# Making the low part of streamed fp32 weights by an accumulating DMA in place of a GpSimd subtraction

## The chip, the cores and the metric

The kernel runs on one core of a Trainium2 chip. The metric is the device time of one execution in microseconds (us). The time of the kernel before is the median of three runs.

## The reference

One inference step of a two-layer trunk in fp32, for a prompt of 16 + 1024 tokens and for eight sample sequences of eight tokens each. Layer 0 mixes tokens by gated DeltaNet, layer 1 by RWKV-7; both are wrapped in RMSNorm and a residual add. Cut to its dense products, which are what the change touches:

```python
# layer 0, D = 1024, 16 value heads of 128
xn   = rmsnorm(x, norm_w[0])
proj = xn @ w_in                        # 1024 x 6176: q, k, v, z and two gates
qkv, z = causal_conv(proj[..., :4096]), proj[..., 4096:6144]
o    = delta_rule(qkv, gates)           # chunked, state 128 x 128 for each head
x    = x + (rmsnorm(o) * silu(z)) @ w_out           # 2048 x 1024
# layer 1, 16 heads of 64
xn   = rmsnorm(x, norm_w[1])
r, k, v, z = [mix(xn, i) @ w_rkvz[i] for i in range(4)]   # 4 x 1024 x 1024
y    = wkv(r, k, v, decay, a)           # state 64 x 64 for each head
x    = x + (groupnorm(y) * silu(z)) @ w_o           # 1024 x 1024
```

## The kernel before, in words

All 1104 tokens (64 of the samples, 16 meta, 1024 of the prompt) stand as columns in three segments of 384, 384 and 336. Activations lie in SBUF as a high part, rounded to the `fp32r` type that TensorE reads, and a low part, the rest. A dense product sums three products, high weight by high activation, low weight by high activation and high weight by low activation, into one PSUM tile (`dense`, line 208; `dense3`, line 1067, for some projections).

Weights are streamed by `load_w` (line 189). A *weight tile* is 128 output columns; it comes in *halves* of four contraction blocks, each a tile of 128 partitions by 4 x 128 numbers (256 KB). For each half:

- SyncE loads the raw fp32 half from DRAM into `wraw` (line 197, two buffers);
- ScalarE casts it to the high part `whi` (line 82 in `split`, three buffers);
- GpSimd subtracts, raw less high, into the low part `wlo` (line 86 in `split`, three buffers).

With three buffers for the low part, the second half of a tile takes the buffer of the first half of the tile before. A buffer is free when TensorE has used it in the last of the three segments. Calls of `load_w` with `into` (16 halves of the second part of `gdn_w_out`, and two halves that are loaded again) let VectorE subtract, into tiles that stay; the change leaves them as they are. Without `into` there are 260 halves: 96 of `gdn_w_in`, 20 of `gdn_w_out`, 96 of `rwkv_w_rkvz` and 48 of `rwkv_w_o`. Four of the 20 are the two tiles that the second part of `gdn_w_out` starts with.

The stages in order: the input's norm; for each of eight pairs of heads `j` the projections for keys (PSUM tile `dk`), queries (`dq`), two values (`dv`) and two gates (`dz`), between which the inverse of a triangular matrix runs on VectorE (`inverse32`, lines 439 and 441) and the recurrence of the pair before on all engines; the output projection (`d`, lines 906 and 914); the norm and token shift of layer 1; the RWKV projections (`project`, line 1138); the gates (`rwkv_gates`, line 1020: `dz` for the first segment, `zz` for the others, one segment at a time); the RWKV recurrence with the output projection (`project_out`, line 1521) interleaved; the final norm.

The order of the instructions on each engine is not written out by hand: the kernel is built with a scheduler that plans it from its own cost model (`schedule_with_timeline_sim=True`, line 1779). Each engine then runs its list in order and waits at its head. So an instruction that comes late holds up all that stands behind it on its engine, and a change of one instruction's planned cost reorders the rest.

Of the kernel before, what the change touches and what calls it, by code (L numbers as in the profile page):

```python
# [10 lines left out]
AF = mybir.ActivationFunctionType  # L11
ALU = mybir.AluOpType
# [23 lines left out]
class Builder:  # L36
# [152 lines left out]
    def load_w(self, src, kt=8, into=None):  # L189

        nc = self.nc
        n = src.shape[1]
        v = src.rearrange("(k p) m -> p k m", p=128)
        his, los = [], []
        for h in range(0, kt, 4):
            w = self.t(self.wp, [128, 4, 128], "wraw", 2)
            nc.sync.dma_start(w[:, :, 0:n], v[:, h:h + 4, :])
            if into:
                hi, lo = into[0][h // 4], into[1][h // 4]
            else:  # L200
                hi = self.t(self.wp, [128, 4, 128], "whi", 3, F32R)
                lo = self.t(self.wp, [128, 4, 128], "wlo", 3, F32R)
            self.split(w[:, :, 0:n], hi[:, :, 0:n], lo[:, :, 0:n], eng_lo="dve" if into else "pool")
            his.append(hi)
            los.append(lo)
        return his, los
# [1576 lines left out]
```

## Time and profile before

| | |
|---|---|
| Median of three runs | 2455.74 us (2452.48 to 2456.87) |
| The profiled execution | 2463.55 us |
| Its span, first to last instruction | 2461.6 us |
| Granted TensorE clock, mean | 0.972 |
| Busy: TensorE, VectorE, ScalarE, GpSimd | 93%, 67%, 56%, 44% |
| Bytes moved by DMA | 284.66 MB, all from SyncE's queue but 3.38 MB of instructions |

PE is TensorE's matmul, PEld its weight load, DVE is VectorE, ACT ScalarE, POOL GpSimd, SP SyncE; a `q` behind the name is that engine's instruction queue. L86 is line 86 of the kernel. `wlo<-wraw,whi` names the tile written and those read, buffer numbers left out. A group's row has its count, its busy time in us, the mean of one in ns, the idle time of its engine just before it, and what ended most of that. In the timeline a row has start and duration in us; merged rows carry a count. The rows of a matmul overlap the next one's, since matmuls are pipelined: what counts for pace is the distance between two starts.

### The profile page before, as it was taken

What the parts mean: (1) busy time and instruction counts of PE and PEld (TensorE: products, weight loads), DVE (VectorE), ACT (ScalarE), POOL (GpSimd) and SP (SyncE); (2) the same over time, 40 slices, a digit from 0 to 9 for tenths busy, and PEclk for the clock granted to TensorE, in tenths of its full rate; (3) what the DMA queues carried; (4) which work ended last, traced back from release to release, by engine and by line L of the source; (5) the groups of instructions that cost most, each with busy time, mean ns of one, the idle gap of its engine ahead of it and who ended that gap; (6) DMA issues with size and microseconds to landing.
All of it is one profiled execution on the core that took longest, in us unless ns stands there. A gap on an engine that the chain in (4) does not pass through costs nothing. (4 is left out here: it accounts for less than half of the span.)

```text
span 2461.6 us, 52742 instructions
## 1 busy us (share of the span) xinstructions
PE 2285.6 (93%) x18593; PEld 2053.9 (83%) x18593; DVE 1657.3 (67%) x4364; ACT 1370.1 (56%) x3817; POOL 1090.5 (44%) x1478
## 2 busy tenths in 40 slices
PE   6989999999999999999999999988979999999996
PEld 5888989898988989889899998876758777877885
DVE  6878676876768586843358344788865687667563
ACT  5455546564555564664336465564434577677663
POOL 3435343433444343441315235433357565656653
PEclk9999999999999999999999999999989999999997
DMA  3323333333332424261531556667565443343331
GB/s 109 103 72 99 84 108 84 102 86 85 88 101 66 118 81 106 73 203 57 150 94 42 168 178 168 165 192 179 148 197 166 125 139 107 91 142 89 109 103 49
DMA packets 471939, 284.66 MB, mean 116 GB/s; under 512 B 187481, under 2 KB 457050, under 8 KB 471674
## 3 DMA queue, kind: packets, MB, share of 16 engines
q1 hardware_dynamic: 471674, 281.29, 40.5%
q8 instruction: 147, 2.41, 0.4%
q14 instruction: 118, 0.97, 0.1%
HBM read 200.00 MB, written 81.17 MB: 114 GB/s over the span
## 5 line engine op out<-in xcount | busy, mean ns | idle before, releaser
L86 POOL TENSOR_TENSOR wlo<-wraw,whi 128x512 fp32r<-128x512 f32 x260 | 349.0, 1346 | 369.4 <-ACT whi L82 334.9
L82 ACT CAST whi<-wraw 128x512 fp32r<-128x512 f32 x260 | 160.0, 617 | 162.0 <-PE dq L76 50.6
L76 PE MATMUL d<-xc,whi 128*128 128x384 f32 (+3 forms) x846 | 239.0, 340 | 1.8 <-ACT ev L1145 1.8
L406 DVE SCALAR_TENSOR_TENSOR cvy<-raw,cw,cvy 128x408 f32<-128x408 f32 (+2 forms) x288 | 176.7, 626 | 16.6 <-ACT cvy L62 14.8
L439 DVE TENSOR_TENSOR invtmp<-invA,invT 72x31 f32<-72x31 f32 (+31 forms) x403 | 163.5, 406 | 17.0 <-POOL invT L434 6.4
L441 DVE TENSOR_TENSOR invT<-invT,invtmp 72x31 f32<-72x31 f32 (+31 forms) x403 | 169.0, 419 | 6.4
L76 PEld LDWEIGHTS d<-xc,whi 128*128 128x128 f32 (+1 forms) x846 | 155.5, 191 | 9.6 <-issue 5.3
L76 PE MATMUL dz<-xc,whi 128*128 128x384 f32 (+1 forms) x480 | 149.5, 343 | 0.0
L76 PE MATMUL dv<-xc,whi 128*128 128x384 f32 (+1 forms) x480 | 146.7, 334 | 0.0
L76 PE MATMUL d<-xa,whi 128*128 128x384 f32 (+3 forms) x450 | 139.0, 342 | 3.4 <-ACT xa L82 2.5
L76 PE MATMUL dz<-xa,whi 128*128 128x384 f32 (+1 forms) x416 | 136.8, 350 | 2.9 <-ACT whi L82 2.6
L76 PE MATMUL d<-xc,wlo 128*128 128x384 f32 (+2 forms) x396 | 131.2, 341 | 0.0
L855 POOL TENSOR_SCALAR Sb<-Sb,eglb 128x128 f32<-128x128 f32 x128 | 80.2, 645 | 88.5 <-DMA Sb<-in_state_gdn 23.1
L76 PE MATMUL rA<-rS,AR 128*64 128x128 f32 x512 | 106.8, 291 | 7.4 <-DVE rS L1432 4.4
L76 PE MATMUL rA<-UV,G 128*64 128x64 f32 x1152 | 112.5, 223 | 0.4 <-ACT UV L62 0.4
L76 PEld LDWEIGHTS rA<-UV,G 128*64 128x64 f32 x1152 | 101.9, 139 | 3.2 <-issue 1.4
L76 PE MATMUL dv<-xa,whi 128*128 128x384 f32 (+1 forms) x288 | 99.9, 347 | 0.1
L62 ACT ACTIVATE rX<-rA,rk 64x64 f32<-64x64 f32 x272 | 83.6, 307 | 23.0 <-PE rA L76 17.1
L76 PE MATMUL dz<-xa,wlo 128*128 128x384 f32 (+1 forms) x256 | 89.8, 351 | 5.3 <-POOL wlo L86 5.3
L1432 DVE SCALAR_TENSOR_TENSOR rS<-rA,DC,pre 64x64 f32<-64x64 f32 x256 | 72.2, 282 | 28.2 <-PE rA L76 22.5
L76 PE MATMUL fG<-AR,BK 128*128 128x128 f32 x576 | 86.3, 288 | 4.4 <-DVE G L1366 2.3
L76 PEld LDWEIGHTS dz<-xc,whi 128*128 128x128 f32 x480 | 89.7, 192 | 0.8
(506 smaller groups left out, 7500.1 us busy)
## 6 DMA issues: line engine op xcount, KB each, us to landing
wraw<-in_gdn_w_in SPq DMA_DIRECT2D x96, 256.0 KB
wraw<-in_rwkv_w_rkvz SPq DMA_DIRECT2D x96, 256.0 KB
Sb<-in_state_gdn SPq DMA_DIRECT2D x64, 256.0 KB
wraw<-in_rwkv_w_o SPq DMA_DIRECT2D x48, 256.0 KB
E<-drow SPq DMA_DIRECT2D x24, 384.0 KB
attn<-drow SPq DMA_DIRECT2D x24, 384.0 KB
wraw<-in_gdn_w_out SPq DMA_DIRECT2D x36, 256.0 KB
out_s_gdn<-Sb SPq DMA_DIRECT2D x32, 256.0 KB
```

Of the source, the lines that this page charges most:

```text
L62: return self.nc.scalar.activation(out, in_, func, bias=bias, scale=scale, **kw)
L76: self.nc.tensor.matmul(out, lhsT, rhs, start=start, stop=stop)
L82: nc.scalar.copy(hi, x)
L86: e.tensor_tensor(lo, x, hi.bitcast(F32), op=ALU.subtract)
L406: nc.vector.scalar_tensor_tensor(y[:, 0:wd], raw[:, k:k + wd], cw[k], y[:, 0:wd], op0=ALU.mult, op1=ALU.add)
L439: nc.vector.tensor_tensor(tmp, A[:, j, j + 1:32].unsqueeze(2).broadcast_to([nb, n, m]), Tv[:, j, 0:m].unsqueeze(1).broadcast_to([nb, n, m] ...
L441: nc.vector.tensor_tensor(Tv[:, j + 1:32, 0:m], Tv[:, j + 1:32, 0:m], tmp, op=ALU.subtract)
L855: nc.gpsimd.tensor_scalar(Sb[:, u], Sb[:, u], self.eglb[:, hv, 4 * g + u:4 * g + u + 1], None, op0=ALU.mult)
L1432: nc.vector.scalar_tensor_tensor(S[hs[h], h, :], dS, DC[hs[h], ci:ci + 1], pre[hs[h], hs[h]], op0=ALU.mult, op1=ALU.add)
```

## The change

Where a half has no `into`, the split is written out in three steps. ScalarE still casts the high part. ScalarE then writes the negated raw half into the low tile, whose type is `fp32r`, so that the tile holds the negated high part. Then GpSimd issues a DMA that reads the raw weights from DRAM a second time and adds them onto that tile. The sum is raw less high, as before. GpSimd's subtraction goes away; 260 ScalarE instructions and 260 DMAs of 256 KB come in. `wraw` is now read by two ScalarE instructions and by none of GpSimd.

```diff
             else:
                 hi = self.t(self.wp, [128, 4, 128], "whi", 3, F32R)
                 lo = self.t(self.wp, [128, 4, 128], "wlo", 3, F32R)
-            self.split(w[:, :, 0:n], hi[:, :, 0:n], lo[:, :, 0:n], eng_lo="dve" if into else "pool")
+            if into:
+                self.split(w[:, :, 0:n], hi[:, :, 0:n], lo[:, :, 0:n], eng_lo="dve")
+            else:
+                nc.scalar.copy(hi[:, :, 0:n], w[:, :, 0:n])
+                self.act(lo[:, :, 0:n], w[:, :, 0:n], AF.Identity, scale=-1.0)
+                nc.gpsimd.dma_start(lo[:, :, 0:n], v[:, h:h + 4, :], accum_op=ALU.add)
             his.append(hi)
             los.append(lo)
```

Lines behind 203 stand five further down in the changed kernel: the cast is line 206, the DMA line 208.

The scheduler makes a new order on every engine. The place shown is a weight tile in the middle of the first output projection, at 1135 to 1141 us of the profile before, on TensorE. Before, the first half of the tile is `whi_15073` and `wlo_15074`, the second `whi_15079` and `wlo_15080`, and `d_15083` is the sum of the first segment:

```order
L76 MATMUL d_15083<-xa_111,whi_15073 128x384
L76 MATMUL rA_14360<-X_14362,TT_16_126 128x128
L76 MATMUL d_15083<-xa_111,wlo_15074 128x384
L76 MATMUL d_15083<-xc_115,whi_15073 128x384
L76 MATMUL d_15083<-xc_115,whi_15079 128x384
L76 MATMUL d_15083<-xc_115,wlo_15080 128x384
L76 MATMUL d_15083<-xa_111,whi_15079 128x384
L76 MATMUL d_15083<-xc_115,whi_15079 128x384
```

In the changed kernel the halves are `whi_15082`, `wlo_15083` and `whi_15089`, `wlo_15090`; `d_15094` is the sum of the first segment and `d_15121` that of the second:

```order
L76 MATMUL d_15094<-xc_115,whi_15089 128x384
L76 MATMUL rA_14356<-X_14358,TT_15_125 128x128
L76 MATMUL rA_14355<-S_14101,Q_13372 128x128
L76 MATMUL rA_14355<-w_14359,attn_14201 128x128
L76 MATMUL rA_14355<-w_14359,ktok_14337 128x128
L73 MATMUL mktok_14486<-ident_74,K_12843 128x128
L76 MATMUL d_15121<-xa_111,whi_15082 128x384
L76 MATMUL d_15121<-xa_111,wlo_15083 128x384
L76 MATMUL d_15121<-xc_115,whi_15082 128x384
L76 MATMUL d_15121<-xa_111,whi_15082 128x384
L76 MATMUL d_15121<-xa_111,wlo_15083 128x384
L76 MATMUL d_15094<-xc_115,wlo_15090 128x384
```

The first matmul with the second half's low part no longer follows at once on that with its high part: matmuls of the recurrence and the start of the next segment's sum now stand in between.

On ScalarE the cast of the same half (`whi_15079` before, `whi_15089` after) stands among the recurrence's instructions, before first and then after:

```order
L62 ACTIVATE w_14316<-rA_14312,nbp_12898 128x128
L62 ACTIVATE ojunk_14335,ssq_14207<-o_14310 128x128
L82 CAST whi_15079<-wraw_15077 128x512
L62 ACTIVATE o_14310<-rA_14312,gcol_131 128x128
L82 CAST whi_15164<-wraw_15162 128x512
```

```order
L62 ACTIVATE ojunk_14333,ssq_14303<-o_14304 128x128
L62 ACTIVATE wlo_15090<-wraw_15087 128x512
L206 CAST whi_15089<-wraw_15087 128x512
L62 ACTIVATE w_14359<-rA_14355,nbp_12984 128x128
L62 ACTIVATE wlo_15176<-wraw_15173 128x512
```

Here the negation went ahead of the cast; in the new order it does so for 183 of the 260 halves, and for 77 it comes behind.

On GpSimd the DMA stands where the subtraction stood, in one queue with the other work:

```order
L86 TENSOR_TENSOR xa_111<-K_14627,xc_115 128x336
L86 TENSOR_TENSOR xc_115<-Q_14629,xc_115 128x336
L208 DMA wlo_15083<-in_gdn_w_out 128x4x128
L571 AFFINE_SELECT attn_14390<-attn_14390 128x768
L99 TENSOR_TENSOR ors_14342<-ovar_14340,cvals_79 128x6
L208 DMA wlo_15090<-in_gdn_w_out 128x4x128
```

Of these six instructions the two DMAs are the new kind; each is held at its place until ScalarE's negation of that half is done.

## The prediction

> **What bounds the kernel now.** I read the page first, then the waits of TensorE, the busy times by stage, and last the timeline around single weight halves.
>
> ```profile
> span 2461.6 us, 52742 instructions
> PE 2285.6 (93%) x18593; PEld 2053.9 (83%) x18593; DVE 1657.3 (67%) x4364; ACT 1370.1 (56%) x3817; POOL 1090.5 (44%) x1478
> q1 hardware_dynamic: 471674, 281.29, 40.5%
> L86 POOL TENSOR_TENSOR wlo<-wraw,whi 128x512 fp32r<-128x512 f32 x260 | 349.0, 1346 | 369.4 <-ACT whi L82 334.9
> L82 ACT CAST whi<-wraw 128x512 fp32r<-128x512 f32 x260 | 160.0, 617 | 162.0 <-PE dq L76 50.6
> L855 POOL TENSOR_SCALAR Sb<-Sb,eglb 128x128 f32<-128x128 f32 x128 | 80.2, 645 | 88.5 <-DMA Sb<-in_state_gdn 23.1
> ```
>
> TensorE is busy for 93% of the span, so it is the bound nearly everywhere, and the kernel gets longer by whatever new time TensorE stands still. The subtraction that goes away is 349 us of GpSimd, which is idle more than half of the time. What TensorE waits for today (waiter, releaser, us in all, times, longest):
>
> ```profile
> PE r L73 <- DVE x L269: 20.7, 3, 15.0
> PE rA L76 <- ACT rX L62: 6.2, 14, 1.3
> PE dz L76 <- POOL wlo L86: 5.3, 6, 1.2
> PE fbpp L73 <- DMA invR<-rssd: 4.0, 3, 1.7
> PE d L76 <- POOL wlo L86: 2.4, 3, 0.9
> ```
>
> These are the largest row of each engine, and both rows of `wlo`. In all, 25 rows with VectorE as releaser add up to 81 us, 28 with ScalarE to 40, 9 with GpSimd to 19, 6 with a DMA to 17. The low parts cost TensorE 7.7 us: they are nearly always in time. So the question is how much later they may come.
>
> **How much slack a low part has.** One weight tile is two halves of four contraction blocks; the pools hold three low halves and three high halves. So the second half of a tile can be made only when TensorE is through with the first half of the tile before. Between that release and the first use lie 26 matmuls of the weights, plus whatever else is interleaved. The timeline of four such places (start, duration; in each pair the last use of the half that is released, then the first use of the new one), and the work between them for the last pair:
>
> ```profile
> 692.80 0.32 PE L76 MATMUL dk<-xa,wlo 128*128 128x336 f32 x1
> 699.12 0.42 PE L76 MATMUL dq<-xc,wlo 128*128 128x384 f32 x1
> 787.48 0.32 PE L76 MATMUL dz<-xa,wlo 128*128 128x336 f32 x1
> 793.41 0.44 PE L76 MATMUL dz<-xc,wlo 128*128 128x384 f32 x1
> 806.74 0.32 PE L76 MATMUL dz<-xa,wlo 128*128 128x336 f32 x1
> 814.95 0.34 PE L76 MATMUL dk<-xc,wlo 128*128 128x384 f32 x1
> 1134.86 0.32 PE L76 MATMUL d<-xa,wlo 128*128 128x336 f32 x1
> 1140.44 0.34 PE L76 MATMUL d<-xc,wlo 128*128 128x384 f32 x1
> 1135.42 0.62 ACT L82 CAST whi<-wraw 128x512 fp32r<-128x512 f32 x1 [0.92 <-issue]
> 1136.12 1.28 POOL L86 TENSOR_TENSOR wlo<-wraw,whi 128x512 fp32r<-128x512 f32 x1 [11.28 <-ACT whi L82]
> ```
>
> From the release (end of the first row of a pair) to the use there are 6.0, 5.6, 7.9 and 5.3 us. In the last pair the low part is ready at 1137.40, 2.2 us after the release, so it has 3 us to spare. Followed through the whole timeline, 98 of the 260 halves have under 9 us: 22 in the DeltaNet stage (three in each of its heads, of the kinds shown), 8 in the first output projection (4.1 to 6.0, mean 5.1), 21 in the RWKV projections (mean 6.7), the rest in the gate and output projections behind. The others have mostly 9 to 40 us, and no delay of a few us touches them.
>
> **The new path, term by term.** Its prices come from these rows: a load of a raw half from SyncE's issue (the first row gives min/median/max of 48 issues) to the cast that waits for it, GpSimd's longest common instruction, and twelve matmuls of one half.
>
> ```profile
> L197 SPq DMA_DIRECT2D wraw<-in_rwkv_w_o x48: 367/384/1437, 1970.5 to 2438.3; - x48
> 2438.29 0.37 SPq L197 DMA_DIRECT2D wraw<-in_rwkv_w_o  x1
> 2441.03 0.62 ACT L82 CAST whi<-wraw 128x512 fp32r<-128x512 f32 x1 [2.00 <-DMA wraw<-in_rwkv_w_o]
> 2442.64 1.84 PE d L76 x12
> 1140.42 1.34 POOL L99 TENSOR_TENSOR ors<-ovar,cvals 128x6 f32<-128x6 f32 x1
> ```
>
> After the release: ScalarE reaches the negation (0.2 us in the last pair; I take 0.5). The negation takes 0.62, like the cast over the same tile (row above). Where the scheduler put it behind the cast it comes 0.62 later, which holds for 77 of 260 in the new order: 0.18 on average. The hand-over to GpSimd is 0.1 (1136.04 to 1136.12). The wait behind other work in GpSimd's queue, between 0.1 and the 1.34 of the row above, is taken as 0.5. Then GpSimd issues the DMA, and the DMA flies.
>
> No DMA issued by GpSimd and no accumulating DMA stands in this trace, so both are bounded by rows. Issue: at least SyncE's 0.38. At most, if GpSimd's own cores write a record for each of the 512 rows of 512 bytes, I price them like its own pass over 128 rows of 512 bytes, 0.645 (the `L855` row): four passes are 2.58 us, eight (source and old value apart) 5.2. I take 2.58, since the DMA's view is 128x4x128, four such passes. Flight: the same 256 KB takes 2.74 us from issue to the waiting cast, 2.37 of it after the issue. One packet takes 0.405 x 16 x 2461.6 / 471674 = 33.8 ns, a half has 512 packets or 32 for each DMA engine, so reading the old value as well adds 1.1 us: 3.5, with a third pass 4.5. I take 3.5.
>
> Release to ready: 0.5 + 0.62 + 0.18 + 0.1 + 0.5 + 2.58 + 3.5 = **8.0 us** (was 2.2). The ends are 0.5 + 0.62 + 0.18 + 0.1 + 0.1 + 0.38 + 2.37 = 4.3 and 0.5 + 0.62 + 0.18 + 0.1 + 1.34 + 5.2 + 4.5 = 12.4.
>
> The Trainium skill (DMA: Bandwidth & Descriptors, Anatomy of one DMA — SWDGE path) fits a DMA issued by GpSimd as about 2.0 us fixed plus bytes over 436 GB/s, with descriptor generation small; by it 256 KB would be an estimated 2.6 us for issue and flight together, the release-to-ready 4.5, and nearly nothing would be lost. No run shown here has such a DMA to agree or not; the fit is for plain copies.
>
> **What the new order gives back.** The scheduler pulls other work ahead of the late low halves; at the pair at 1135 to 1140, seven more matmuls of the weights lie in the window (33 against 26, small ones 9 in both; 1.1 us at 1.84 / 12 each). By kind: the `dq` window gains 5 small matmuls (to some 6.5 us), the `dk` window loses 23 small ones (to 6.0), the last `dz` gains 36 small ones (to 7.5).
>
> **The sum of new stalls at 8.0 us.** DeltaNet: (1.5 + 2.0 + 0.5) x 8 heads = 32. First output projection: windows of 4.1 to 6.0 plus 0.2 to 2.2 gained; of the eight shortfalls one is 3.7, the others 0.4 to 2.0: 11. RWKV projections: 6.7 plus about 1.7 gained, so half of the 21 fall short, by 1 us: 10. The gates of the first segment are this stretch (the instructions on `wlo` alone: busy TensorE, weight load, GpSimd, with counts):
>
> ```profile
> 1766.00:1822.00 56.00, 23.31 (x65) 12.56 (x65) 20.88 (x15) 0.97 0.60 158
> ```
>
> Three buffers go round, each held 8.0 us and then the 2 us of its twelve matmuls, so one half each 3.3 us; the stretch makes 15 in 56 us, 3.7 each: 0. Later gates: eight windows are under 8.0, short by 10 us, but a half comes every 2 us of work there and one stall serves the next half too: 5. Last output projections: 24 short ones, mean 6.4, shared in the same way: 24 x 1.6 / 2 = 19. Together 77 us.
>
> Beside it: 260 negations add 160 us to ScalarE, 12% of its busy time; the 40 us that TensorE waits for it grow alike, +5. GpSimd goes from 1090 to 741 + 671 = 1412 us; its other 11 us of TensorE waits grow by 30%, +3. The new packets (260 x 512 x 33.8 ns / 16 = 281 us, doubled, 23% on a share of 40.5%) stretch other transfers; the 17 us of DMA waits grow by 23/40, +10. VectorE is held up less:
>
> ```profile
> 508.18 2.66 POOL L86 TENSOR_TENSOR wlo<-wraw,whi 128x512 fp32r<-128x512 f32 x2 [4.13 <-ACT whi L82]
> 509.75 1.32 DVE L441 TENSOR_TENSOR invT<-invT,invtmp 72x207 f32<-72x207 f32 x1
> 511.49 0.35 DVE L441 TENSOR_TENSOR invT<-invT,invtmp 72x192 f32<-72x192 f32 x1
> L441 DVE TENSOR_TENSOR invT<-invT,invtmp 72x207 f32<-72x207 f32 x16 | 12.5, 779 | 0.4
> L441 DVE TENSOR_TENSOR invT<-invT,invtmp 72x192 f32<-72x192 f32 x16 | 5.8, 363 | 0.4
> ```
>
> An instruction that takes 0.35 us took 1.32 while GpSimd subtracted, ending as GpSimd ends. One VectorE instruction held for half a subtraction, 0.67 us, 260 times, when VectorE has work (67%): 117 us of VectorE, 7%, and of TensorE's 81 us of waits for it 6: -6. The Trainium skill (SBUF — State Buffer, Who interferes with whom) says a VectorE instruction with two SBUF inputs and a GpSimd one that reads SBUF exclude each other for a whole instruction; this trace agrees, 1.32 against 0.35 us. SyncE's waits have this row:
>
> ```profile
> SPq L197 <- POOL wlo L86: 321.7, 120, 15.6
> ```
>
> The raw tile is now released by ScalarE's 0.62 instead of GpSimd's 1.35, so SyncE, whose queue stands for 322 us before these loads, moves a little earlier; no raw load is short of time where the low part isn't, so I give it nothing.
>
> Sum: 77 + 5 + 3 + 10 - 6 = 89 us. The profiled execution took 2463.55 us (span 2461.6), 7.8 above the median of the three; I add the 89 to the median: 2455.74 + 89 = 2545 us.
>
> **Rivals.** *The DMA is dear* (18%): issue 5.2 and flight 4.5. Release to ready nears 11.7. The DeltaNet heads then lack 5.7 + 5.2 + 4.2 and two more windows 6 together, 21 x 8 = 169; the first projection 8 x 5.2 = 42, RWKV's 21 x 3.3 = 69, the gates 15 x 0.9 + 13 x 4.2 / 2 = 41, the last projections 24 x 5.3 / 2 = 64: 385. GpSimd holds 741 + 260 x 5.2 = 2093 us, which stretches its 11 us of waits by 10, the third pass takes 5 more on DMA waits: 5 + 10 + 15 - 6 = 24 beside it, 2865 us. For it: a half is 512 separate rows on each side; against: SyncE needs 0.38 for the same rows.
>
> *Faster* (12%): the lower end, 4.3 us, is under nearly all windows (only one of the first projection's eight is shorter). Then no stall stays, the 7.7 us of waits for `wlo` go, VectorE's relief gives 6, ScalarE takes 5: -9, 2447 us; with VectorE's relief twice as large on the way, 2441. It decides below about 5 us from release to ready. By the skill's fit above it would come out so.
>
> *No change within 0.2%* (5%; 0.2%, about 5 us, is what a measurement of this kernel can tell): 5 to 5.5 us, where the first projection's few us of stalls balance the relief. That the DMA is not what is waited for is excluded: 260 of them stand in GpSimd's queue in the new order, and the low part's first matmul waits for them.
>
> **Chances and range.** The forecast, stalls at the second halves, has 65%, on its own from 2480 (6 us, where DeltaNet lacks nothing and the rest about 12) to 2760 (10.5 us, two thirds of the way to the dear case). The range from 2441 to 2790 takes in most of the faster case and leaves out most of the dear one. Slower by over 0.2%: 65 + 18 = 83%; faster 12%; the same 5%.
>
> **What the profile after would show.** Right: a GpSimd row for the DMA of `wlo` with a mean near 2.6 us; TensorE waits with the DMA of `wlo` as releaser, 60 to 100 us in all, largest for `dq`, `dk`, `dz` and `d`; ScalarE up by 160; VectorE's busy time down by about 117; the 72x207 row near 0.38. Wrong: those waits under 20 us (then the lower end holds), or GpSimd's row at 5 us and more, or TensorE waiting instead for GpSimd's other work or for `whi`.

## The result, and the profile after

The changed kernel takes 2612.21 us (median of four runs, 2606.68 to 2619.54), against 2454.36 us for the kernel before: 1.0634 times as long, 95% interval 1.0612 to 1.0656, or 158 us. The profiled execution of the changed kernel has a span of 2605.2 us, 143.6 more than the profile of before.

The page's head, busy times and DMA queues of the changed kernel:

```profile
span 2605.2 us, 53138 instructions
PE 2336.1 (90%) x18593; PEld 2088.3 (80%) x18593; DVE 1565.9 (60%) x4364; ACT 1509.1 (58%) x4077; POOL 1086.6 (42%) x1478
q1 hardware_dynamic: 471674, 281.29, 38.8%
q0 software_dynamic: 137280, 68.17, 21.6%
```

Its span and mean granted clock:

```profile
core 0: 2605.2 us, clock 0.957
```

TensorE stands still for 2605.2 - 2336.1 = 269.1 us, 93 more than before (2461.6 - 2285.6 = 176.0). But its busy time has grown too, by 50.5 us, at the same 18593 matmuls. The clock tells why: of the span (1 - 0.957) x 2605.2 = 112 us were withheld, (1 - 0.972) x 2461.6 = 69 before, 43 more. So of the 143.6 us, 93 are standing still and 43 are a slower TensorE; some 8 are left over.

What TensorE waits for in the changed kernel (all rows of the low part over 1 us, then the largest of the others that grew):

```profile
PE dk L76 <- DMA wlo<-in_gdn_w_in: 16.7, 6, 3.4
PE rY L76 <- DMA T1n<-g_t: 16.0, 7, 2.9
PE d L76 <- DMA wlo<-in_rwkv_w_rkvz: 15.3, 8, 3.5
PE fss L73 <- POOL Q L423: 12.2, 6, 3.6
PE dz L76 <- DMA wlo<-in_rwkv_w_rkvz: 9.6, 6, 4.2
PE d L76 <- DMA wlo<-in_rwkv_w_o: 8.5, 8, 3.1
PE fsr L76 <- POOL kqm L832: 7.0, 5, 1.8
PE zz L76 <- DMA wlo<-in_rwkv_w_rkvz: 6.5, 2, 5.8
PE d L76 <- DMA wlo<-in_gdn_w_out: 6.3, 3, 3.5
PE dz L76 <- DMA wlo<-in_gdn_w_in: 2.7, 1, 2.7
```

With two rows under 1 us the low part makes 66.1 us, where GpSimd's subtraction made 8.8 (5.3 and 2.4 in the rows shown, and 1.1 in a third, of `zz`). By releaser, all rows together: DMA 17 to 100 us, ScalarE 40 to 54, GpSimd 19 to 35, VectorE 81 down to 64.

One such wait in the timeline: the release of a low buffer (the row at 419.38 is its last use), the negation, the DMA's issue, and the matmul that waited, with the last work before it and one matmul behind it:

```profile
419.38 0.32 PE L76 MATMUL dz<-xa,wlo 128*128 128x336 f32 x1
420.14 1.56 ACT L62 ACTIVATE E<-E,gcol 128x128 f32<-128x128 f32 x5
421.60 0.62 ACT L62 ACTIVATE wlo<-wraw 128x512 fp32r<-128x512 f32 x1
422.51 1.35 POOL L208 DMA_DIRECT2D wlo<-in_gdn_w_in  x1 [2.13 <-ACT wlo L62]
424.43 0.44 PE L76 MATMUL dk<-xc,whi 128*128 128x384 f32 x1
428.17 0.44 PE L76 MATMUL dk<-xc,wlo 128*128 128x384 f32 x1 [3.30 <-DMA wlo<-in_gdn_w_in]
430.52 0.53 PE L76 MATMUL dk<-xc,whi 128*128 128x384 f32 x1
```

Released at 419.70, used at 428.17: 8.5 us, of which 1.9 until ScalarE gets to it, 1.35 the issue, and 4.3 from the issue's end to the first use. The wait itself is 3.30 us. Then comes the part that I had not counted. The busy times of the stretches around it (length, TensorE, weight load, VectorE, ScalarE and GpSimd with counts, granted clock, DMA share, GB/s):

```profile
426.00:429.40 3.40, 1.23 (x7) 1.23 (x8) 0.00 (x0) 0.88 (x4) 2.96 (x5) 1.00 1.32 215
429.40:432.80 3.40, 3.40 (x13) 3.40 (x12) 0.48 (x1) 1.18 (x3) 0.39 (x2) 0.50 0.26 32
432.80:436.00 3.20, 3.20 (x22) 3.20 (x21) 2.03 (x4) 0.55 (x1) 0.00 (x0) 1.00 0.00 0
```

In the 3.4 us behind the wait the clock is 0.50, and TensorE, busy throughout, starts 13 matmuls where the next stretch has 22. The trace of before has 28 such stretches, the changed one 42, each of 3.4 us or a few times that.

The Trainium skill (TensorE: Matmul & The Clock Gate, Part 1: The HAM clock gate) says that the clock is either full or half, goes to half after an idle window of about 3.4 us and comes back after a busy one. The traces agree in the half and in the 3.4 us. They differ in what it takes: at 1130.05 us a stand of 1.50 us, with TensorE busy before and behind it, was followed by 3.4 us at 0.50, while one of 1.26 us at 1264.03 us was not.

The length of a stand alone does not decide it, though. This one of 3.09 us cost no clock (the matmul that waited, then three stretches, columns as above):

```profile
567.49 0.44 PE L76 MATMUL dk<-xc,wlo 128*128 128x384 f32 x1 [3.09 <-DMA wlo<-in_gdn_w_in]
562.53:565.94 3.41, 1.87 (x10) 1.34 (x8) 0.69 (x2) 3.41 (x12) 1.85 (x2) 1.00 0.63 109
565.94:569.36 3.42, 1.87 (x11) 1.87 (x11) 0.00 (x0) 0.19 (x1) 2.36 (x4) 1.00 1.26 199
569.36:572.77 3.41, 3.41 (x22) 3.41 (x22) 1.72 (x3) 1.18 (x3) 0.39 (x2) 1.00 0.02 2
```

In each trace all stretches of 0.50 begin on one grid of 3.41 us, and a line of this grid, at 565.94, cuts the stand into 1.54 and 1.55 us. Take the steps of this grid at full clock, in both traces without the first 30 us. After a step in which TensorE stood for less than 0.9 us the clock never fell (748 steps). After one with 1.9 us or more it always did (40 steps). In between it fell after 29 of 105. So one and the same stand can cost no clock, or half of 3.41 us, by where it falls.

The price of the DMA, by the lines of negation, cast and DMA on the page, and the median from issue to landing:

```profile
L62 ACT ACTIVATE wlo<-wraw 128x512 fp32r<-128x512 f32 x260 | 163.3, 628 | 98.1 <-PE d L76 20.2
L208 POOL DMA_DIRECT2D wlo<-in_rwkv_w_rkvz x96 | 125.0, 1330 | 156.2 <-ACT wlo L62 135.7
L208 POOL DMA_DIRECT2D wlo<-in_gdn_w_in x96 | 127.9, 1361 | 140.9 <-ACT wlo L62 132.4
wlo<-in_gdn_w_in POOLq DMA_DIRECT2D x96, 256.0 KB, 5.8
```

GpSimd is held for 1.33 to 1.36 us by each issue in these rows, about as long as by the subtraction (1.346), so its busy time has hardly moved (1086.6 us, 1090.5 before). A packet of this queue takes 0.216 x 16 x 2605.2 / 137280 = 65.6 ns; SyncE's take 34.3 in the same way, 33.8 before. These are means over all sizes; packets of 512 bytes alone take 67 ns here and 30 ns in SyncE's queue.

The Trainium skill's fit (DMA: Bandwidth & Descriptors, Anatomy of one DMA — SWDGE path), an estimated 2.6 us for these 256 KB, is less than half of the 5.8 measured. The Trainium skill calls the generation of descriptors small there; GpSimd is held by the issue for 1.3 of the 5.8.

### The profile page after: what moved, and what is told of

The parts are those of the page before. It is cut to its first block, busy times and chain, and to the rows that moved or that the text cites. A ratio compares the mean times of both kernels' runs of the same rounds, so it can differ in the third digit from the quotient of the medians.

```text
span 2605.2 us, 53138 instructions
## 1 busy us (share of the span) xinstructions
PE 2336.1 (90%) x18593; PEld 2088.3 (80%) x18593; DVE 1565.9 (60%) x4364; ACT 1509.1 (58%) x4077; POOL 1086.6 (42%) x1478
## 3 DMA queue, kind: packets, MB, share of 16 engines
q0 software_dynamic: 137280, 68.17, 21.6%
## 5 line engine op out<-in xcount | busy, mean ns | idle before, releaser
L62 ACT ACTIVATE wlo<-wraw 128x512 fp32r<-128x512 f32 x260 | 163.3, 628 | 98.1 <-PE d L76 20.2
L411 DVE SCALAR_TENSOR_TENSOR cvy<-raw,cw,cvy 128x384 f32<-128x384 f32 (+2 forms) x288 | 171.4, 608 | 61.1 <-ACT cvy L62 59.9
L208 POOL DMA_DIRECT2D wlo<-in_rwkv_w_rkvz x96 | 125.0, 1330 | 156.2 <-ACT wlo L62 135.7
L208 POOL DMA_DIRECT2D wlo<-in_gdn_w_in x96 | 127.9, 1361 | 140.9 <-ACT wlo L62 132.4
L446 DVE TENSOR_TENSOR invT<-invT,invtmp 72x31 f32<-72x31 f32 (+31 forms) x403 | 143.1, 355 | 6.9
L76 PE MATMUL dz<-xa,whi 128*128 128x384 f32 (+1 forms) x416 | 144.1, 370 | 2.6 <-ACT whi L206 2.6
L444 DVE TENSOR_TENSOR invtmp<-invA,invT 72x31 f32<-72x31 f32 (+31 forms) x403 | 141.9, 352 | 7.1 <-POOL invT L439 0.5
L860 POOL TENSOR_SCALAR Sb<-Sb,eglb 128x128 f32<-128x128 f32 x128 | 89.7, 747 | 77.9 <-DMA Sb<-in_state_gdn 45.2
L76 PEld LDWEIGHTS d<-xa,whi 128*128 128x128 f32 (+1 forms) x450 | 86.1, 195 | 10.1 <-issue 4.7
L76 PE MATMUL d<-xa,wlo 128*128 128x384 f32 (+3 forms) x252 | 87.7, 348 | 6.9 <-DMA wlo<-in_rwkv_w_rkvz 6.9
```

The lines of the kernel that those rows point to most:

```text
L62: return self.nc.scalar.activation(out, in_, func, bias=bias, scale=scale, **kw)
L76: self.nc.tensor.matmul(out, lhsT, rhs, start=start, stop=stop)
L208: nc.gpsimd.dma_start(lo[:, :, 0:n], v[:, h:h + 4, :], accum_op=ALU.add)
L411: nc.vector.scalar_tensor_tensor(y[:, 0:wd], raw[:, k:k + wd], cw[k], y[:, 0:wd], op0=ALU.mult, op1=ALU.add)
L444: nc.vector.tensor_tensor(tmp, A[:, j, j + 1:32].unsqueeze(2).broadcast_to([nb, n, m]), Tv[:, j, 0:m].unsqueeze(1).broadcast_to([nb, n, m] ...
L446: nc.vector.tensor_tensor(Tv[:, j + 1:32, 0:m], Tv[:, j + 1:32, 0:m], tmp, op=ALU.subtract)
```

## The experiments

The theory after this reading: the low half comes 8 us after the release of its buffer, TensorE stands where it is needed sooner, and each stand of some length costs again by the halved clock. The rivals: GpSimd's issue time and the doubled packets slow everything, wherever they stand; or ScalarE's negations do. Ratios are to runs of the kernel before on the same chip.

**The same program with a plain copy.**

```diff
-                nc.gpsimd.dma_start(lo[:, :, 0:n], v[:, h:h + 4, :], accum_op=ALU.add)
+                nc.gpsimd.dma_start(lo[:, :, 0:n], v[:, h:h + 4, :])
```

> The changed kernel with a plain copy in place of the accumulation (the low part is then the raw weight, no remainder; the negation stays and is overwritten). Theory (late halves): the copy's packets need no read of the old value; 33 packets per DMA engine at about 34 instead of 66 ns make the landing some 1 us earlier, so the waits for wlo fall by 20 to 30 us and the clock loss with them by about half as much: 2565 to 2590 us; GpSimd's row stays at 1.3 us. If the accumulation itself is the cost: under 2500 us. If only the issue by GpSimd and the fixed way matter: 2605 us or more.

The scheduler made the same order for this kernel as for the changed one, on every engine, so nothing but the DMA differs. 2508.6 us, ratio 1.0195 (1.0147 to 1.0242); the profile has a span of 2505.6, 99.6 less than the changed kernel's. Its page, with busy times, queue, one group of the DMAs and their landing:

```profile
PE 2303.5 (92%) x18593; PEld 2063.9 (82%) x18593; DVE 1559.1 (62%) x4364; ACT 1507.4 (60%) x4077; POOL 949.3 (38%) x1478
...
q0 software_dynamic: 137280, 68.17, 14.9%
...
L208 POOL DMA_DIRECT2D wlo<-in_gdn_w_in x96 | 74.5, 776 | 155.4 <-ACT wlo L62 146.2
...
wlo<-in_gdn_w_in POOLq DMA_DIRECT2D x96, 256.0 KB, 4.2
```

Its span and clock:

```profile
core 0: 2505.6 us, clock 0.969
```

The issue is 0.78 us instead of 1.36, the packet 0.149 x 16 x 2505.6 / 137280 = 43.5 ns instead of 65.6, the landing at 4.2 instead of 5.8. Followed over all halves whose negation starts within 3 us of the release, release to landing is 6.4 us on average instead of 8.1. These 1.8 us were worth 99.6: TensorE stands 202.1 us (67 less) and the clock loss is (1 - 0.969) x 2505.6 = 78 us (34 less). TensorE's waits for the low part go from 66.1 to 19.5, those for GpSimd from 35 to 21: 47 and 14 of the 67 us. I had expected the late halves to give 22 to 47 us. The time fell twice as far, to near the value that I gave for the accumulation itself as the cost (under 2500 us), and the issue moved, which no theory had. As the order is the same, this shows that what the accumulating DMA takes longer than a plain copy, in issue and flight, is the larger part of the 158 us. In this comparison each microsecond of standing came with another half by the clock (34 to 67), as between before and after (43 to 93).

**A fourth low buffer.** In the space there was, it could be had up to the first output projection, with one staging tile in place of two, so it has a control of the same layout with three buffers.

```diff
-                lo = self.t(self.wp, [128, 4, 128], "wlo", 3, F32R)
+                lo = self.t(self.wl, [128, 4, 128], "wlo", self.nl, F32R)
...
-        self.l0 = pool("layer0", ctx)
+        self.l0, self.wl, self.nl = pool("layer0", ctx), pool("wl0", ctx), 4
...
-        sb = [t(sp, [128, 512], f"stage{k}") for k in range(2)]
+        sb = [t(sp, [128, 512], f"stage{k}") for k in range(1)]
...
+        self.wl, self.nl = pool("wl1", top), 3
...
+        self.wl = rpool("wl2", ctx)
```

> The changed kernel with a fourth low buffer up to the first output projection, so that a half no longer waits for a buffer of the tile just before (to make room, the low tiles lie in pools of their own and the input of the residual has one staging tile for two). Theory (the low half starts only at the release of a buffer and then needs 8 us): TensorE's waits for wlo in the DeltaNet stage and the first projection fall from about 29 us to under 6, and against the same layout with three buffers the kernel is 35 to 70 us faster. Rival (the low half is late for another reason: GpSimd's queue, the raw load, the DMA queues): less than 15 us.

> The control for the fourth buffer: the changed kernel with the same pools and one staging tile, but three low buffers. 2590 to 2630 us, waits for wlo of 55 to 75 us.

> The kernel before in that layout (pools of their own, one staging tile, three low buffers). It does the same work, but the scheduler plans it anew: if a new plan alone costs nothing, 2450 to 2470 us; if a new plan alone is worth what the negation alone cost, it lies 20 to 40 us off, either way.

With four 2583.86 us (1.0512, 1.0484 to 1.0539), with three 2635.34 (1.0719, 1.0691 to 1.0747; a little above the 2590 to 2630 that I gave it): 51 us, inside the expected 35 to 70. TensorE's waits for the DeltaNet weights' low parts, with three buffers:

```profile
PE dk L76 <- DMA wlo<-in_gdn_w_in: 17.7, 6, 3.4
PE dz L76 <- DMA wlo<-in_gdn_w_in: 4.6, 2, 3.1
PE dv L76 <- DMA wlo<-in_gdn_w_in: 0.2, 1, 0.2
```

With four, no row of `in_gdn_w_in` is left, and the last `dv` matmul ends at 1045 us instead of 1087: 42 us for 22.5 us of waits. With GpSimd's subtraction in the same layout it ends at 1027, so the fourth buffer gave back 42 of the 60 us that this stage had lost. The rest of the kernel, where three buffers stay, did not change its pace. So it is the wait for the buffer that makes these halves late, not the raw load or the queues; the orders of the two kernels differ too, but the waits that went are the ones that a buffer more should end. The subtraction in this layout takes 2479.16 us (1.0088, 1.0066 to 1.0110), 23 us more, at the lower edge of the second case that I gave. Little of it is the plan: from the last `dv` to the last `dlora` matmul (`lora_first`, line 1100) it takes 344 us, 326 before, and there, with one staging tile, TensorE waits 12.6 us for the loads of `stage`, 2.3 before. That cost falls on both sides of the comparison, and is about what the control is slower than the changed kernel.

**First halves or second halves.** Only halves with `h` = 0, or only those with `h` = 4, go by the DMA.

```diff
-            if into:
+            if into or h:        # the second kernel: if into or not h
-                self.split(w[:, :, 0:n], hi[:, :, 0:n], lo[:, :, 0:n], eng_lo="dve")
+                self.split(w[:, :, 0:n], hi[:, :, 0:n], lo[:, :, 0:n], eng_lo="dve" if into else "pool")
```

> Only the first half of each weight tile (130 of the 260) goes by the DMA; the second halves are subtracted by GpSimd as before. Theory (late second halves: about 8 us from the release of a low buffer to the landing, felt only where the half is needed within that time, and each stall of over about 1.5 us halves TensorE's clock for 3.4 us or more): TensorE's waits for the DMA of wlo fall from 66 us to under 15, the clock loss from 113 us to under 85, time 2460 to 2490 us. Rival (GpSimd's issue time, the extra packets and ScalarE's negations slow the kernel wherever they stand, in proportion to their number): half of the 158 us, about 2533 us.

> The counterpart with the same number of DMAs, negations and subtractions: only the second halves go by the DMA, the first are subtracted. Theory (late second halves): TensorE's waits for the DMA of wlo stay at 45 to 66 us, the clock loss at 95 to 113 us, time 2560 to 2610 us. Rival (cost in proportion to the number): about 2533 us, the same as with the first halves.

The counts are 138 and 122, since 16 tiles of `rwkv_w_o` have one half only. First halves: 2515.16 us, 1.0211 (1.0172 to 1.0250). Second halves: 2520.61, 1.0235 (1.0196 to 1.0274). The same within the intervals, as the rival has it, though both lie under its value (half of 6.3% would be 3.2%). My theory was wrong in its place, and both times and both clock losses lie outside what I gave for it. Waits for the DMA of the low part are 17.5 and 48.3 us, as I expected within a few us, and the DeltaNet stage goes as I thought (last `dv` matmul at 1039 and 1048 us, before 1027). But with the first halves the waits stand in the gates and the last projections:

```profile
PE d L76 <- DMA wlo<-in_rwkv_w_o: 8.6, 6, 3.3
PE dz L76 <- DMA wlo<-in_rwkv_w_rkvz: 5.0, 3, 2.8
PE zz L76 <- DMA wlo<-in_rwkv_w_rkvz: 3.9, 1, 3.9
```

There a half comes every 2 to 4 us, and by these rows first halves are late too. By the granted clocks (0.961 and 0.966) the clock loss was 98 us with the first halves and 86 with the second (69 before). What of it is lateness and what the negations' and the new order's, this pair doesn't tell.

**The negation alone.** The kernel before, with ScalarE's negation into the low tile, which GpSimd's subtraction then overwrites; in the text ahead of the cast, of one column only, or behind the cast.

```diff
+            if not into:
+                self.act(lo[:, :, 0:n], w[:, :, 0:n], AF.Identity, scale=-1.0)   # or [:, :, 0:1]
             self.split(w[:, :, 0:n], hi[:, :, 0:n], lo[:, :, 0:n], eng_lo="dve" if into else "pool")
```

In the third of them the two lines of `split` are written out, and the negation stands between them.

> The kernel before, with ScalarE's negation of the raw half written into the low tile first and then overwritten by GpSimd's subtraction: the 260 extra ScalarE instructions without any DMA, and the low part some 0.7 us later at most. Theory (late halves): 0 to +12 us, 2455 to 2467 us. Rival (ScalarE's 160 us more are what costs): over +40 us, 2495 us or more.

> The negation alone once more, but of one column in 128 (about 0.2 instead of 0.63 us of ScalarE each): 260 more instructions, a third of the time, and a new plan. If the 35 us of the full negation are ScalarE's time on the path: 2460 to 2475 us. If they are the new plan's, they need not shrink: 2480 to 2500 us.

> The negation alone, in full width, but behind the cast of the high half (as the changed kernel has it) and ahead of GpSimd's subtraction, which overwrites it. If the 35 us of the negation alone came from the cast's being 0.63 us later: 2460 to 2478 us, and that is the negation's share in the changed kernel. If they came from ScalarE's 160 us more: 2490 to 2500 us again.

Full width 2498.17 us (1.0134, 1.0089 to 1.0179); one column 2466.11 (1.0034, 1.0014 to 1.0053); behind the cast 2489.08 (1.0120, 1.0081 to 1.0159). So the negation by itself costs about 1.2%, 30 us, six times what I gave it. The one column has as many instructions and a new order of its own, and costs 0.3%; so most of the 30 us goes with ScalarE's time, as far as orders that differ can be compared. Where the text puts the negation made no clear difference: the scheduler put it ahead of the cast for 214 of 260 halves in the first kernel, for 169 in the third (183 in the changed kernel). Whether it costs less strictly behind the cast was not tried. In the last kernel two of TensorE's rows that grew are these (5.5 and 2.6 us before):

```profile
PE rA L76 <- DVE X L757: 8.8, 15, 1.3
PE dz L76 <- ACT whi L206: 6.4, 6, 1.9
```

**A quarter of the DMA.** One contraction block of four, or 32 columns of 128.

```diff
-                nc.gpsimd.dma_start(lo[:, :, 0:n], v[:, h:h + 4, :], accum_op=ALU.add)
+                nc.gpsimd.dma_start(lo[:, 0:1, 0:n], v[:, h:h + 1, :], accum_op=ALU.add)
# the other kernel
+                nc.gpsimd.dma_start(lo[:, :, 0:32], v[:, h:h + 4, 0:32], accum_op=ALU.add)
```

> The changed kernel with a DMA of only one of the four contraction blocks of a half: 128 rows of 512 bytes in place of 512 (the other three blocks of the low part keep the negated high part). If issue and flight go by rows: GpSimd's row falls from 1.33 to 0.4 to 0.7 us, the flight from 4.9 to 3.0 to 3.6, release to landing from 8.1 to about 5.7, the time to 2475 to 2510 us. If both are fixed: 1.3 us and over 4.5 us, 2580 us or more.

> The same quarter of the bytes in as many rows as the full DMA: 512 rows of 128 bytes (the other columns of the low part keep the negated high part). If the price goes by rows: GpSimd's row 1.3 us, release to landing over 7.3 us, 2560 us or more. If it goes by bytes: the same as one block of four.

What the DMA leaves out stays the negated high part here, so these kernels show times and make no usable low part. Both came out faster than the kernel before, which neither theory had: 2450.07 us (0.9937, 0.9914 to 0.9960) and 2450.46 us (0.9961, 0.9942 to 0.9980). One block, from the page and from the list of its DMAs:

```profile
L208 POOL DMA_DIRECT2D wlo<-in_gdn_w_in x96 | 86.4, 903 | 198.7 <-ACT wlo L62 178.7
```

```profile
wlo<-in_gdn_w_in POOLq DMA_DIRECT2D x96, 64.0 KB, 3.7
```

The columns, from the same two views:

```profile
q0 software_dynamic: 137280, 17.06, 12.3%
...
L208 POOL DMA_DIRECT2D wlo<-in_gdn_w_in x96 | 128.2, 1361 | 183.2 <-ACT wlo L62 179.7
```

```profile
wlo<-in_gdn_w_in POOLq DMA_DIRECT2D x96, 64.0 KB, 4.5
```

The issue goes by rows and not by bytes: 1.36 us for 512 rows of 128 bytes as for 512 of 512, and 0.90 for 128 rows, so that a part of it is fixed. What follows it goes more by bytes: 2.8 and 3.1 us for 64 KB against 4.4 for 256 (landing less issue). The columns' kernel has the negations, 260 issues of the full length and as many packets as the changed kernel, and is faster than before. So the number of issues and of packets is not what makes the changed kernel slow. Against the negation alone (1.0120) the columns' kernel is 1.6%, 39 us, faster, although TensorE now waits 24.6 us for the DMA. What sets the two apart is that GpSimd no longer subtracts, and a new order: the scheduler plans a smaller DMA, so both kernels of this section have an order of their own.

How much an order may be worth shows in the step from the columns to the plain copy of 256 KB (2.3%, 57 us). The low part is no later in the plain copy: 4.2 us from issue to landing against 4.5 here, 6.2 us from release to landing against 6.7 (followed through the DeltaNet stage), and TensorE waits 19.5 us for it against 24.6. Nor do the four times as many bytes stretch SyncE's packets: 34.5 and 34.6 ns. TensorE's waits for the DMA of `T1n` differ (16.9 us in the plain copy, under 3 with the columns). So lateness does not explain this step. What is left is mainly the order, but no run changes it alone. And since an order may be worth as much as that, the 39 us above can't be put down to the missing subtraction alone.

**VectorE subtracts.** These runs point to a kernel without the negation, the DMA and GpSimd's subtraction.

```diff
-            self.split(w[:, :, 0:n], hi[:, :, 0:n], lo[:, :, 0:n], eng_lo="dve" if into else "pool")
+            self.split(w[:, :, 0:n], hi[:, :, 0:n], lo[:, :, 0:n], eng_lo="dve")
```

> A version that keeps the relief and drops the negation and the DMA: VectorE subtracts the low part of all 260 halves itself (0.69 us each by its row on the same tile size, 180 us in all; the 91 us that it was held up by GpSimd's subtraction go). If that relief is what made the kernels with a quarter of the DMA faster: 2430 to 2455 us. If VectorE's net 90 us more lie on the path as the negation's 135 us did: 2465 to 2490 us.

2451.88 us, 0.9956 (0.9933 to 0.9980): 0.4% faster than the kernel before, inside the first range that I gave, and so 6% faster than the changed one. A new order is in the 0.4% too. Its busy times and VectorE's new row:

```profile
PE 2271.0 (93%) x18593; PEld 2055.3 (84%) x18593; DVE 1731.8 (71%) x4624; ACT 1375.0 (56%) x3817; POOL 775.5 (32%) x1218
L86 DVE TENSOR_TENSOR wlo<-wraw,whi 128x512 fp32r<-128x512 f32 x260 | 191.2, 736 | 104.7 <-ACT whi L82 99.6
```

VectorE takes on 191 us and is busy for only 74 more than before, which fits that its other instructions are no longer held; TensorE's waits for it fall from 81 to 61 us.

## Why the prediction was right in kind and short in size

Slower by the late halves was forecast, +89 us, and came, +158, inside the range. What the sum adds up is nearly all standing, and TensorE stands 93 us more: that this is so near to 89 is luck, since too much was given to the low part and too little to the rest. By steps, the forecast against what the profile after and the runs show (waits in TensorE's rows):

| step | forecast | measured |
|---|---|---|
| release to ready | 8.0 us | 8.1 us |
| TensorE's waits for the low part | 77 us | 66 us, and the 8.8 of before gone |
| TensorE's clock | not in the sum | 43 us |
| the negation | +5 us | +14 us in ScalarE's rows; 30 us by itself |
| GpSimd's other work | +3 us | +25 us |
| other transfers | +10 us | +17 us |
| VectorE held up less | -6 us | -17 us |

- *Release to ready* was right by luck, as a sum of two wrong terms. The issue was taken as 2.58 us and is 1.35; the flight was taken as 3.5 and is 4.8. Four passes of GpSimd over its partitions were no measure of the issue, and a second read of the old value no measure of a packet of 512 bytes that takes 67 ns instead of 30.
- *The waits* came out for `dk` as priced in their sum (16.7 us in six waits for eight times 2.0), and for `dq` not at all (0.3 us for eight times 1.5). The waits of before, which go, were taken as 7.7 us from two rows and left out of the sum; the third row, 1.1 us, was missed. By stage they are 20, 6, 15, 16 and 9 us (DeltaNet, first projection, RWKV, gates, last), against 32, 11, 10, 5 and 19. The gates, which I priced at almost nothing by their cycle of 3.7 us, were the worst misjudged.
- The step that failed most is the first: "the kernel gets longer by whatever new time TensorE stands still". It gets longer by that and by the clock that is lost behind it, 43 us here. The trace of before showed a clock of 0.972 and where it was 0.50; I read the mean and did not ask what brought it down. The half that the clock added here is no fixed price: against before, the negation alone, ahead of the cast in the text, makes TensorE stand 18 us more with no more clock loss, and the first halves 34 us more with 29 us of clock loss.
- *The negation* was priced through TensorE's 40 us of waits for ScalarE, raised by 12%. Alone it costs 30 us. TensorE's rows with ScalarE grew by 14 us in the changed kernel and by 7 to 8 in the kernels with the full negation alone, where its rows with VectorE grew by 9 to 11: ScalarE's lateness shows up in other engines' rows too.
- *GpSimd's other work* was priced by GpSimd's being busy for 1412 us; it is busy for 1087, as long as before. Of the 25 us, 19 stand at `Q` and `kqm`. These stand behind the scaling of `Sb` in GpSimd's queue, which takes longer (747 ns, 645 before) and whose own wait for the DMA of `Sb` grew from 23 to 45 us. Of *other transfers*, the largest is `T1n`: from the issue of `g_t` to the first matmul that uses `T1n` it takes 7.3 us before and 6.6 after, as medians of the eight pairs of heads, and SyncE's packets went from 33.8 to 34.3 ns. So for `T1n` not the transfer is longer but the work above it thinner; contention, as I priced it, does not show there. That these rows come from the new order is argued from this, not shown by a run that undoes it.
- *VectorE's relief* is seen where I looked for it: the 72x207 row is at 0.375 us, as forecast, from 0.779:

```profile
L446 DVE TENSOR_TENSOR invT<-invT,invtmp 72x207 f32<-72x207 f32 x16 | 6.0, 375 | 0.4
```

VectorE is busy for 91 us less (117 forecast). What that is worth I probably had too low, because I scaled TensorE's direct waits for VectorE, and not what they set off: the rows alone give 17 us, and the columns' kernel is 39 us faster than the one with GpSimd's subtraction. With orders that differ, the second is not shown to be the relief alone.

- The *faster* rival set its point at 5 us from release to ready. No such point shows: the columns' kernel is faster than before with 6.7 us in the DeltaNet stage, the plain copy 2% slower with 6.2. So at this size something besides lateness decides; the orders differ between the two, and the forecast had no term for the order.

Put together as ratios: the negation +1.2%; GpSimd's subtraction gone and a quarter of the DMA in, -1.6%; 256 KB as a plain copy, +2.3%; the accumulation, +4.4%. Only the last step is at equal order and so shown as a cause; in each of the others a new order is mixed in, and how they divide among lateness, relief and order stays open.

## What to carry to other kernels

Where TensorE is the bound, ask what a stand does to the clock behind it: here the clock added 43 us to 93 us of standing. List the stands that a change adds with their lengths and places, not only their sum. A step moved into a DMA is as late as its issue and its flight, and what decides is the time from the release of its buffer to the first use; measure that at the tight places, or give it a buffer more. Ask what an engine's work does to its neighbours before giving it away: VectorE, which GpSimd's subtraction had held up, took on 191 us of that work and was busy for only 74 more, and the kernel got no slower. Where a scheduler makes a new order for every change, compare at equal order, as the plain copy allowed, before a difference of 1 or 2% is put down to a cause.

## What the runs showed of the hardware

- TensorE's clock falls to 0.50 for 3.41 us or a multiple, on a grid of 3.41 us: in the traces before and after, without their first 30 us, always behind a step with 1.9 us or more of standing (40 of 40), never behind one with under 0.9 us (748 steps). A stand of 1.50 us inside one step was enough, one of 3.09 us across two was not.
- A DMA of 512 rows issued by GpSimd holds GpSimd for 0.78 us as a plain copy, and for 1.36 us with an accumulation, whether its rows have 128 or 512 bytes; 128 rows with accumulation 0.90.
- Its packets of 512 bytes take 67 ns when they accumulate and 44 when they only copy; those of SyncE's queue take 29 to 30.
- A VectorE instruction that reads two tiles (72x207) takes 0.779 us on average in the kernel with GpSimd's subtraction and 0.375 in the changed one; one of 72x207 that ran during a subtraction took 1.32.
